# A hybrid decoder block: HGRN2's products inside blocks of 32 tokens in four partition ranges, and probabilities by values for two heads in turn

## The chip, the cores and the metric

The kernel runs on one core of a Trainium2 chip. The metric is the device time of one execution in microseconds (us), the median of three runs. All tensors are fp32; the large projections split each operand into a high and a low part and multiply those, so that each is several passes on TensorE. A matmul of fp32 operands shows as two MATMUL records and two LDWEIGHTS records in the trace (a product of 128x128 by 128x128 is one instruction in the code and two records).

## The reference, cut to what matters

One decoder layer on x (1024 tokens, 1024 wide): an RMSNorm, one combined projection, three groups of heads, an output projection, and a gated feed-forward part. The two groups that the change touches most:

```python
def hgrn2_mix(q, f_logit, i, g, lb, out_gain):      # 4 heads, keys and values 128 wide
    log_f = jnp.logaddexp(jnp.log(lb), jnp.log1p(-lb) + jax.nn.log_sigmoid(z))
    k = (1.0 - lb) * jax.nn.sigmoid(-z)
    ...
        b = jnp.cumsum(gc, axis=2)
        o_inter = jnp.einsum('bhck,bhkv->bhcv', qc * jnp.exp(b), S)
        decay = jnp.exp(jnp.where(causal[:, :, None], diff, -jnp.inf))
        A = jnp.einsum('bhtk,bhtsk,bhsk->bhts', qc, decay, kc)
        o = o_inter + jnp.einsum('bhts,bhsv->bhtv', A, vc)
        S = jnp.exp(b_last[:, :, 0, :])[..., None] * S + ...

def dsa_mix(...):                                    # 4 heads of 64, 256 keys kept per query
    logits = jnp.einsum('bqhd,bqkhd->bhqk', qb, kg) * (SA_DH ** -0.5)
    p = jax.nn.softmax(jnp.where(valid[:, None], logits, -jnp.inf), axis=-1)
    return jnp.einsum('bhqk,bqkhd->bqhd', p, vg)

x = x + (mixed @ w_out[layer]);  x = x + ((silu(a) * b) @ w_ffn_out[layer])
```

The third group, memory attention (`mem_mix`), is the same softmax attention over 256 memory tokens.

## The kernel before

Lines are those of the kernel before. A framework with a scheduler takes the program in the order of its code, simulates the engines, and sets from that the order in which each engine's queue holds its instructions; buffers come from pools by tag. PSUM has the tags `mm`, `lg`, `rc` and `sm`, two banks of 128x512 each; the large SBUF tiles are `x0` to `x17` and `m0` to `m7`, one buffer each.

The stages, by time in the trace: projections and the indexer's scores to 150 us; memory attention from there to about 280; the HGRN heads and, beside them, two bisections that find the 256th largest score of each query (blocks of queries 7 and 4 counted on VectorE, L635; blocks 6, 5, 3 and 2 on ScalarE, L632); sparse attention from about 553 to 703 with HGRN head 3 in front of it and among it; the output projection (`wo`) from 620 to 793; then the feed-forward part (`ff`, `fo`) to the end, which the change does not touch.

**HGRN levels.** A head is 1024 tokens in 8 chunks of 128. `hgrn_intra` (L504 to L554) builds A, the decayed products of keys and queries inside a chunk, by levels. Q (queries), K (keys) and F (decays) lie with the 128 key dimensions on the partitions and 1024 tokens along them. Level 0 is the diagonal; five more levels with w = 1, 2, 4, 8, 16 fill in the pairs that lie in opposite halves of a block of 2w tokens; w = 32 and 64 are done apart (L542). In each of the six products `level_products` (L511) multiplies all of a chunk's 128 keys by all of its 128 queries, 8 matmuls of 128x128 in two banks of `rc`, although a level uses only pairs at most 31 tokens apart. VectorE takes from it what belongs to the level: by a product with the identity (L528) for the diagonal and by `copy_predicated` under a mask (L535) for the others, each in two instructions of 128x512. Between the products `descend` scales Q on VectorE (L521), K on GpSimd (L522) and F on VectorE (L523), one half of the tokens at a time. So a level is a loop: matmuls read Q and K, then Q and K are overwritten, then the next level's matmuls read them.

Heads 0 to 2 run through `hgrn_intra` as the program order comes to them (279 to 330, 391 to 427, 459 to 513 us), among projections of other heads; head 3 is put among the sparse attention's steps by `fillers`, and its levels stand in front of nearly all of them (553 to 571 us).

**Sparse attention.** 32 items, one for each block b of 128 queries (7 down to 0) and head h. An item goes through logits (L819, L821), the exponential (L830), a scale by GpSimd (L836), transposes of the 128x128 blocks of probabilities on TensorE (L845) with copies to a tile `PT` (L848, L850), and `sa_out`: for each of the b+1 blocks of keys a matmul of 64 columns (L857) into partitions 0 to 63 (even head) or 64 to 127 (odd head) of a bank, and a copy of 64x128 by ScalarE (L859). The bank has the tag `mm` at first (tile names `sat_mm`) and `rc` later (`sat_rc`).

The memory attention's L711 does the same for its two blocks of memory tokens, head j outside and block kb inside.

Of the kernel before, what the change touches and what calls it, by code (L numbers as in the profile page):

```python
# [42 lines left out]
def hybrid_block(ctx, tc, xT, memT, wch, wikw, wv, wkm, wvm, woa, wob, wfi, wfo,  # L43
# [23 lines left out]
    def bank(tag):  # L67

        return pp.tile([128, 512], F32, tag=tag, name=nm(tag))
# [13 lines left out]
    def bs(b):  # L83
        return slice(b * 128, b * 128 + 128)
# [18 lines left out]
    lv = held(160).bitcast(U8).rearrange("p (a b) -> p a b", a=5)  # L103
# [196 lines left out]
    G.tensor_copy(lv, lvf)  # L300
# [203 lines left out]
    def hgrn_intra(h):  # L504
        s, Q, K, F, Gt, A = heads[h]
        idb = ident.unsqueeze(1).to_broadcast([128, 4, 128])

        def level_products(hf):
            rc = bank("rc")
            for c in range(4):  # L510
                T.matmul(rc[:, bs(c)], K[:, bs(4 * hf + c)], Q[:, bs(4 * hf + c)], start=True,  # L511
                         stop=True)
            return rc.rearrange("p (a b) -> p a b", a=4)
# [11 lines left out]
        lg = [level_products(hf) for hf in range(2)]  # L525
        for hf in range(2):
            V.tensor_mul(Q[:, hs(hf)], Q[:, hs(hf)], F[:, hs(hf)])
            V.tensor_mul(A[:, 4 * hf:4 * hf + 4], lg[hf], idb)  # L528
        yield
        for i in range(5):  # L530
            mask = lv[:, i, :].unsqueeze(1).to_broadcast([128, 4, 128])
            lg = [level_products(hf) for hf in range(2)]
            for hf in range(2):
                descend(1 << i, hf)
                V.copy_predicated(A[:, 4 * hf:4 * hf + 4], mask, lg[hf])  # L535
            yield
        for w in (32, 64):
# [139 lines left out]
    def memory_attention():  # L677
        ph[0] = "mat"
        Pm, PTm = mt(2, (128, 2, 2, 256)), mt(3, (128, 2, 2, 2, 128))
        for b in range(8):  # L680
            for m in range(2):
# [26 lines left out]
                for j in range(2):  # L708
                    h = 2 * m + j
                    for kb in range(2):  # L710
                        T.matmul(po[ROWS[j], 0:128], vm[:, kb, 64 * h:64 * h + 64], PT[:, j, kb, :],  # L711
                                 start=kb == 0, stop=kb == 1)
# [138 lines left out]

    def sa_out(t):
# [423 lines left out]
```

## Time and profile before

| | us |
|---|---|
| median of 3 runs | 1437.39 (1437.28 to 1437.59) |
| profiled execution, its own time | 1437.38 |
| span of that execution | 1435.6 |
| TensorE busy | 1331.7 (93%) |
| VectorE busy | 1062.5 (74%) |
| ScalarE busy | 685.2 (48%) |
| GpSimd busy | 462.4 (32%) |
| mean granted TensorE clock | 0.97 of full speed |

The profiled execution is 1.8 us longer than its span and agrees with the median to 0.01 us. In the rows below PE is TensorE, PEld its weight loads, DVE VectorE, ACT ScalarE, POOL GpSimd; Lnnn is a line of the kernel. "x16" in a row counts records; a busy TensorE includes the time that matmuls overlap one another, and a record's own duration says nothing of the rate, which is read from a burst's duration divided by its records. The share of 93% is a mean over stages with different limits: in one stage TensorE is busy without a gap, in the next it waits for VectorE.

### The profile page before, as it was taken

The page shows a single profiled execution, that of the slowest core. Times are in us where ns is not written, and L with a number is a line of the kernel's source. Part 1 is how long each engine was busy: PE and PEld are TensorE (multiplying, and loading weights), DVE is VectorE, ACT ScalarE, POOL GpSimd, SP SyncE. Part 2 cuts the span into 40 slices and gives each one's busy share as a digit, 9 for nine tenths or more (in the row PEclk, how much of TensorE's full clock was granted, in tenths as well). Part 3 has the DMA queues.
Part 4 walks back from the last instruction along what each step waited for, and adds up shares of the span by engine and source line. Part 5 has one row for each costly group of instructions (what it writes and reads, how often), then busy time and mean ns, then how long its engine had stood idle before and what let it go on. Part 6 is the DMA issues. An engine that isn't in the chain of part 4 may idle for free.

```text
span 1435.6 us, 19694 instructions
## 1 busy us (share of the span) xinstructions
PE 1331.7 (93%) x6920; PEld 1103.6 (77%) x6920; DVE 1062.5 (74%) x2119; ACT 685.2 (48%) x1350; POOL 462.4 (32%) x380
## 2 busy tenths in 40 slices
PE   7989999989999978999992999999999998899998
PEld 5767887779888867878771788888888886688887
DVE  8787998895496789654489578777777766666764
ACT  7565789857732252544543333333333333344442
POOL 1401034363365533211115133333332310903630
PEclk9999999999999997999995999999999999899999
DMA  6211011000101000011331232323333249543331
GB/s 229 74 30 30 16 45 31 30 22 27 56 17 45 19 18 32 31 34 48 103 118 58 74 109 97 103 102 103 103 110 110 97 138 352 197 165 101 103 110 59
DMA packets 50643, 120.08 MB, mean 84 GB/s; under 512 B 5744, under 2 KB 5872, under 8 KB 50544
## 3 DMA queue, kind: packets, MB, share of 16 engines
q1 hardware_dynamic: 50256, 118.61, 24.8%
q8 instruction: 54, 0.88, 0.3%
q14 instruction: 45, 0.37, 0.1%
q10 hardware_dynamic: 288, 0.22, 0.0%
HBM read 90.23 MB, written 28.57 MB: 83 GB/s over the span
## 4 chain that ended last, share of the span: by engine, by line
PE 64%; DVE 20%; ACT 9%; DMA 3%; issue 2%; POOL 0%; DVEq 0%; ACTq 0%; POOLq 0%; SPq 0%
PE ff_lg L1030 16%; PE ff_rc L1030 12%; PE wo_mm L184 4%; PE fo_mm L1172 4%; PE fo_sm L1172 4%; ACT idx_x L632 4%; PE fo_lg L1172 3%; PE fo_rc L1172 3%; DVE idx_x L635 3%; PE hg_mm L184 2%; PE sap_mm L184 2%; PE wo_mm L1006 2%; PE idx_mm L184 1%; PE mat_mm L184 1%; PE sat_rc L857 1%
## 5 line engine op out<-in xcount | busy, mean ns | idle before, releaser
L115 ACT ACTIVATE ff_whi<-ff_x 128x512 fp32r<-128x512 f32 x109 | 68.4, 630 | 125.7 <-PE ff_rc L1030 80.2
L1030 PE MATMUL ff_lg<-wo_h,ff_whi 128*128 128x512 f32 x440 | 127.0, 394 | 0.0
L632 ACT ACTIVATE idx_x<-idx_x,packs 128x896 int8<-128x896 f32 (+3 forms) x128 | 105.7, 826 | 44.1 <-DVE packs L627 39.4
L1030 PEld LDWEIGHTS ff_lg<-wo_h,ff_whi 128*128 128x128 f32 x440 | 82.5, 189 | 19.6 <-ACT ff_tmp L1036 2.9
L184 PE MATMUL hg_mm<-xn_h,hg_whi 128*128 128x512 f32 x384 | 96.7, 396 | 0.8 <-DVE hg_x L481 0.8
L1030 PE MATMUL ff_rc<-wo_x,ff_whi 128*128 128x512 f32 x264 | 80.9, 392 | 17.2 <-ACT wo_x L115 17.2
L116 DVE TENSOR_TENSOR ff_wlo<-ff_x,ff_whi 128x512 fp32r<-128x512 f32 x109 | 90.6, 832 | 6.4 <-PE ff_lg L1030 4.4
L1030 PE MATMUL ff_rc<-wo_h,ff_whi 128*128 128x512 f32 x264 | 83.4, 397 | 8.9 <-ACT ff_whi L115 6.6
L184 PEld LDWEIGHTS hg_mm<-xn_h,hg_whi 128*128 128x128 f32 x384 | 71.0, 189 | 15.4 <-DVE hg_x L481 1.0
L1030 PE MATMUL ff_lg<-wo_x,ff_whi 128*128 128x512 f32 x264 | 78.8, 391 | 0.0
L116 POOL TENSOR_TENSOR hg_wlo<-hg_wst,hg_whi 128x512 fp32r<-128x512 f32 x32 | 43.0, 1352 | 104.8 <-ACT hg_whi L115 79.1
L1030 PEld LDWEIGHTS ff_rc<-wo_x,ff_whi 128*128 128x128 f32 x264 | 49.8, 189 | 28.1 <-ACT wo_x L115 17.7
L635 DVE TENSOR_SCALAR_CACHE_REDUCE idx_x<-idx_x,packs 128x1024 int8<-128x1024 f32 x64 | 68.7, 1074 | 0.9
L1030 PE MATMUL ff_lg<-wo_h,ff_wlo 128*128 128x512 f32 x220 | 67.8, 389 | 0.0
L1030 PEld LDWEIGHTS ff_rc<-wo_h,ff_whi 128*128 128x128 f32 x264 | 50.2, 190 | 20.5 <-ACT ff_whi L115 7.0
L511 PE MATMUL hg_rc<-hg_x,hg_x 128*128 128x128 f32 x384 | 53.0, 289 | 11.2 <-POOL hg_x L522 5.7
L511 PEld LDWEIGHTS hg_rc<-hg_x,hg_x 128*128 128x128 f32 x384 | 49.4, 202 | 15.5 <-POOL hg_x L522 7.8
L522 POOL TENSOR_TENSOR hg_x<-hg_x,hg_x 128x256 f32<-128x256 f32 x56 | 45.4, 822 | 43.8 <-PE hg_rc L511 27.1
L1030 PEld LDWEIGHTS ff_lg<-wo_x,ff_whi 128*128 128x128 f32 x264 | 49.7, 188 | 10.7 <-ACT ff_whi L115 0.2
L836 POOL TENSOR_SCALAR sat_x<-sat_x,sat_mz 128x1024 f32<-128x1024 f32 (+7 forms) x32 | 24.1, 755 | 99.6 <-DVE sat_mz L835 80.1
L384 DVE SCALAR_TENSOR_TENSOR idx_x<-idx_tmp,packs,idx_x 128x512 f32<-128x512 f32 (+2 forms) x70 | 46.1, 711 | 12.3 <-ACT idx_tmp L379 11.9
L116 DVE TENSOR_TENSOR fo_wlo<-fo_tmp,fo_whi 128x512 fp32r<-128x512 f32 x33 | 33.5, 1017 | 26.4 <-ACT fo_whi L115 23.7
(445 smaller groups left out, 3722.6 us busy)
## 6 DMA issues: line engine op xcount, KB each, us to landing
gd<-ff_m SPq DMA_DIRECT2D x77, 256.0 KB, 2.0
fo_x<-gd SPq DMA_DIRECT2D x77, 256.0 KB, 3.0
ff_wst<-wfi SPq DMA_DIRECT2D x16, 512.0 KB, 3.6
ff_m<-wfi SPq DMA_DIRECT2D x14, 512.0 KB, 3.6
ff_x<-wfi SPq DMA_DIRECT2D x14, 512.0 KB, 3.7
hg_wst<-wch SPq DMA_DIRECT2D x12, 512.0 KB, 3.6
fo_x<-wfo SPq DMA_DIRECT2D x12, 512.0 KB, 6.4
fo_h<-wfo SPq DMA_DIRECT2D x20, 256.0 KB, 6.0
```

What stands on the lines that cost most here:

```text
L115: S.activation(hi, src, AF.Copy)
L116: (eng or V).tensor_sub(lo, src, hi.bitcast(F32))
L184: T.matmul(ps[:M, :], w(pw, k), h[p][k][hf], start=i == 0, stop=i == len(order) - 1)
L384: V.scalar_tensor_tensor(sc[b][:, c0:c1], rl[:, :c1 - c0], iww[:, b, h:h + 1], sc[b][:, c0:c1], op0=ALU.mult, op1=ALU.add)
L511: T.matmul(rc[:, bs(c)], K[:, bs(4 * hf + c)], Q[:, bs(4 * hf + c)], start=True, stop=True)
L522: G.tensor_mul(Kv[:, :, 0, :], Kv[:, :, 0, :], fr.to_broadcast([128, n, w]))
L632: S.activation(waste[S][:, :nk], sc[b], AF.Sign, bias=nf[:, j:j + 1], accum_out=ct[:, j:j + 1])
L635: eng.tensor_scalar(waste[eng][:, :nk], sc[b], fl[:, j:j + 1], None, op0=ALU.is_ge, op1=ALU.add, accum_out=ct[:, j:j + 1])
L836: G.tensor_scalar(P[:, :nk], P[:, :nk], mx[:, 2:3], 1.0, op0=ALU.mult, op1=ALU.mult)
L1006: T.matmul(ps, wb[k](pw, m), MX[p][KB[k]][hf], start=i == 0, stop=i == 8)
L1030: T.matmul(ps, w[pw][:, bs(k)], HB[u][k][p], start=first and i == 0, stop=i == 11, skip_group_check=True)
L1172: T.matmul(banks[m], w[i][pw][:, bs(m)], b[i][p], start=first and i == 0 and n == 0, stop=i == NP - 1 and n == 2, skip_group_check=True)
```

## The change

`level_products` keeps only what a level can use: for each chunk, four products of 32 keys by 32 queries, one for each block of 32 tokens. The four land in the four partition ranges 0-31, 32-63, 64-95, 96-127 of a PSUM bank, and one bank of 128 x (8x32) holds all eight chunks. There are 32 matmuls (64 records) a level where 8 (16 records) stood, and VectorE takes the level's part in one instruction of 128x256 instead of two of 128x512. After the last level three ScalarE copies a head move the blocks to their places in A and three GpSimd memsets clear what lies beside them. The masks shrink to 32 columns, and eight small copies on GpSimd set up masks and identity once.

In `sa_out` the even head of a pair only keeps its `PT`; the odd head then does both heads' products, alternating between them, and one copy of 128x128 instead of two of 64x128. `L711` alternates the two heads likewise.

```diff
-        idb = ident.unsqueeze(1).to_broadcast([128, 4, 128])
-        def level_products(hf):
+        Ad = A[:, :, 0:32]
+        def level_products():
             rc = bank("rc")
-            for c in range(4):
-                T.matmul(rc[:, bs(c)], K[:, bs(4 * hf + c)], Q[:, bs(4 * hf + c)], start=True,
-                         stop=True)
-            return rc.rearrange("p (a b) -> p a b", a=4)
+            for c in range(8):
+                for o in QUARTERS:
+                    sl = slice(128 * c + o.start, 128 * c + o.stop)
+                    T.matmul(rc[o, 32 * c:32 * c + 32], K[:, sl], Q[:, sl], start=True, stop=True)
+            return rc[:, :256].rearrange("p (c b) -> p c b", c=8)
...
-        lg = [level_products(hf) for hf in range(2)]
+        lg = level_products()
         for hf in range(2):
             V.tensor_mul(Q[:, hs(hf)], Q[:, hs(hf)], F[:, hs(hf)])
-            V.tensor_mul(A[:, 4 * hf:4 * hf + 4], lg[hf], idb)
+        V.tensor_mul(Ad, lg, wide(id32))
         yield
         for i in range(5):
-            mask = lv[:, i, :].unsqueeze(1).to_broadcast([128, 4, 128])
-            lg = [level_products(hf) for hf in range(2)]
+            lg = level_products()
             for hf in range(2):
                 descend(1 << i, hf)
-                V.copy_predicated(A[:, 4 * hf:4 * hf + 4], mask, lg[hf])
+            V.copy_predicated(Ad, wide(lv[:, i, :]), lg)
             yield
+        for o in QUARTERS[1:]:
+            S.activation(A[o, :, o], A[o, :, 0:32], AF.Copy)
+            G.memset(A[o, :, 0:o.start], 0.0)
...
-                for j in range(2):
-                    h = 2 * m + j
-                    for kb in range(2):
+                for kb in range(2):
+                    for j in range(2):
+                        h = 2 * m + j
                         T.matmul(po[ROWS[j], 0:128], vm[:, kb, 64 * h:64 * h + 64], PT[:, j, kb, :],
-                                 start=kb == 0, stop=kb == 1)
+                                 start=kb == 0, stop=kb == 1, skip_group_check=True)
...
     def sa_out(t):
-        b, h, PT, mx = t["b"], t["h"], t["PT"], t["mx"]
+        b, h = t["b"], t["h"]
         m, j = h // 2, h % 2
+        PTs[j] = t["PT"]
+        if j == 0:
+            return
         po = bank(po_tag[0])
         for kb in range(b + 1):
-            T.matmul(po[ROWS[j], 0:128], sv[kb // 4][:, kb % 4, 64 * h:64 * h + 64],
-                     PT[:, kb, :], start=kb == 0, stop=kb == b)
-        S.activation(M[4 + m][ROWS[j], bs(b)], po[ROWS[j], 0:128], AF.Copy)
+            for j in range(2):
+                T.matmul(po[ROWS[j], 0:128],
+                         sv[kb // 4][:, kb % 4, 128 * m + 64 * j:128 * m + 64 * j + 64],
+                         PTs[j][:, kb, :], start=kb == 0, stop=kb == b, skip_group_check=True)
+        S.activation(M[4 + m][:, bs(b)], po[:, 0:128], AF.Copy)
```

The scheduler places the new instructions. In the rows of order below, a row is the line, the operation, the tiles written and read and the shape; "x4" counts instructions of the same kind in a row. Lines of the changed kernel are some higher: L518 are the level products (L511 before), L527, L528 and L529 the descents (L521 to L523), L543 the `copy_predicated` (L535), L546 and L547 the new copies and memsets, L553 the products of w = 32 and 64 (L542), L678 to L686 the steps after the bisections (L667 to L675), L856 the transposes (L845), L875 the products of probabilities and values (L857).

TensorE before, at the end of head 3's levels and the start of sparse attention's output; the rows are of the kernel before.

```order
L511 MATMUL hg_rc_5492<-hg_x_659_4037,hg_x_660_4038 128x128 x4
L511 MATMUL hg_rc_5497<-hg_x_659_4037,hg_x_660_4038 128x128 x4
L845 MATMUL sat_sm_5312<-packs,sat_x_777_5237 128x128 x4
L845 MATMUL sat_sm_5318<-packs,sat_x_777_5237 128x128 x4
L542 MATMUL hg_rc_5583<-hg_x_659_4037,hg_x_660_4038 32x32 x16
L857 MATMUL sat_mm_5370<-sat_x_793_5311,sap_x_557_3000 64x128 x4
L857 MATMUL sat_mm_5370<-sat_x_793_5311,sap_x_558_3001 64x128 x4
```

TensorE at the same place in the changed kernel.

```order
L518 MATMUL hg_rc_6011<-hg_x_641_4458,hg_x_642_4459 32x32 x32
L553 MATMUL hg_rc_6129<-hg_x_641_4458,hg_x_642_4459 32x32 x8
L856 MATMUL sat_sm_5777<-packs,sat_x_759_5658 128x128 x4
L856 MATMUL sat_sm_5783<-packs,sat_x_759_5658 128x128 x4
L553 MATMUL hg_rc_6129<-hg_x_641_4458,hg_x_642_4459 32x32 x8
L553 MATMUL hg_rc_6197<-hg_x_641_4458,hg_x_642_4459 64x64 x4
L856 MATMUL sat_sm_5845<-packs,sat_x_764_5706 128x128 x4
L875 MATMUL sat_mm_5925<-sat_x_773_5776,sap_x_551_3145 64x128
L856 MATMUL sat_sm_5851<-packs,sat_x_764_5706 128x128 x4
```

A level is one burst of 32 small matmuls into one bank, where two times four large ones into two banks stood. The first product of a pair stands by itself among the transposes, before the second head's `PT` is there; a few rows on the rest follow, alternating between the two heads' tiles:

```order
L856 MATMUL sat_sm_5913<-packs,sat_x_769_5761 128x128 x4
L875 MATMUL sat_mm_5925<-sat_x_781_5844,sap_x_551_3145 64x128
L875 MATMUL sat_mm_5925<-sat_x_773_5776,sap_x_551_3145 64x128
L875 MATMUL sat_mm_5925<-sat_x_781_5844,sap_x_551_3145 64x128
L875 MATMUL sat_mm_5925<-sat_x_773_5776,sap_x_551_3145 64x128
```

Every matmul of the pair but the first is next to one of the other head, where a head's whole run stood alone before.

VectorE before, at the end of head 1's levels, where the bisection's last scores are scanned (L672, 896 columns).

```order
L521 TENSOR_TENSOR hg_x_505_2630<-hg_x_505_2630,hg_x_507_2632 128x32x8
L535 COPY_PREDICATED hg_x_530_2820<-packs,hg_rc_3489 128x512
L670 TENSOR_SCALAR packs<-packs 128x1
L523 TENSOR_TENSOR hg_x_507_2632<-hg_x_507_2632 128x32
L521 TENSOR_TENSOR hg_x_505_2630<-hg_x_505_2630,hg_x_507_2632 128x16x16
L535 COPY_PREDICATED hg_x_530_2820<-packs,hg_rc_3502 128x512
L523 TENSOR_TENSOR hg_x_507_2632<-hg_x_507_2632 128x16
L672 SCALAR_TENSOR_TENSOR idx_x_155_801<-idx_x_158_804 128x896
L673 SCALAR_TENSOR_TENSOR idx_x_155_801<-idx_x_155_801,packs,idx_x_158_804 128x896
L674 SCALAR_TENSOR_TENSOR idx_x_155_801<-idx_x_156_802,idx_x_155_801 128x896
L521 TENSOR_TENSOR hg_x_505_2630<-hg_x_505_2630,hg_x_507_2632 128x16x16
L535 COPY_PREDICATED hg_x_530_2820<-packs,hg_rc_3507 128x512
```

VectorE there in the changed kernel (L683 to L685 are the scan and what follows it).

```order
L678 TENSOR_SCALAR idx_x_156_809,packs<-idx_x_155_808,packs 128x896
L527 TENSOR_TENSOR hg_x_499_2775<-hg_x_499_2775,hg_x_501_2777 128x16x16 x2
L543 COPY_PREDICATED hg_x_524_2965<-packs,hg_rc_3757 128x8x32
L681 TENSOR_SCALAR packs<-packs 128x1
L529 TENSOR_TENSOR hg_x_501_2777<-hg_x_501_2777 128x16 x2
L683 SCALAR_TENSOR_TENSOR idx_x_155_808<-idx_x_158_811 128x896
L684 SCALAR_TENSOR_TENSOR idx_x_155_808<-idx_x_155_808,packs,idx_x_158_811 128x896
L685 SCALAR_TENSOR_TENSOR idx_x_155_808<-idx_x_156_809,idx_x_155_808 128x896
L527 TENSOR_TENSOR hg_x_499_2775<-hg_x_499_2775,hg_x_501_2777 128x8x32 x2
```

The last level (w = 16) stands whole in front of the scan, where its second half stood behind the scan and its two followers.

GpSimd before at the same place.

```order
L669 TENSOR_SCALAR idx_x_158_804<-idx_x_155_801,packs 128x896
L522 TENSOR_TENSOR hg_x_506_2631<-hg_x_506_2631,hg_x_507_2632 128x32x8
L522 TENSOR_TENSOR hg_x_506_2631<-hg_x_506_2631,hg_x_507_2632 128x16x16
L669 TENSOR_SCALAR idx_x_158_804<-idx_x_156_802,packs 128x768
L522 TENSOR_TENSOR hg_x_506_2631<-hg_x_506_2631,hg_x_507_2632 128x16x16
L522 TENSOR_TENSOR hg_x_506_2631<-hg_x_506_2631,hg_x_507_2632 128x8x32
```

GpSimd there in the changed kernel.

```order
L680 TENSOR_SCALAR idx_x_158_811<-idx_x_155_808,packs 128x896
L528 TENSOR_TENSOR hg_x_500_2776<-hg_x_500_2776,hg_x_501_2777 128x16x16 x2
L547 MEMSET hg_x_524_2965 32x8x32
L547 MEMSET hg_x_524_2965 32x8x64
L547 MEMSET hg_x_524_2965 32x8x96
L680 TENSOR_SCALAR idx_x_158_811<-idx_x_156_809,packs 128x768
L528 TENSOR_TENSOR hg_x_500_2776<-hg_x_500_2776,hg_x_501_2777 128x8x32 x2
```

The three memsets stand behind the last level's descent and in front of the second L680 and of the descent of w = 32.

## Rows read from the trace of the kernel before

**Rows 1.** The page's first part: busy us, share of span, instructions.
```profile
PE 1331.7 (93%) x6920; PEld 1103.6 (77%) x6920; DVE 1062.5 (74%) x2119; ACT 685.2 (48%) x1350; POOL 462.4 (32%) x380
```

**Rows 2.** Windows by stage: busy us of each engine, granted clock, DMA.
```profile
core 0: us, PE busy (x) PEld busy (x) DVE busy (x) ACT busy (x) POOL busy (x), PEclk, DMA share, GB/s
280.00:330.00 50.00, 42.60 (x263) 38.02 (x261) 49.58 (x111) 26.90 (x59) 28.83 (x23) 0.97 0.11 32
...
391.00:427.00 36.00, 31.48 (x286) 30.28 (x284) 32.25 (x72) 13.12 (x31) 21.31 (x18) 0.99 0.10 30
427.00:517.00 90.00, 89.22 (x545) 77.05 (x544) 65.36 (x164) 24.09 (x43) 41.45 (x39) 0.99 0.10 29
...
553.00:571.00 18.00, 14.66 (x99) 12.97 (x98) 16.62 (x51) 3.79 (x6) 7.72 (x10) 0.92 0.00 0
571.00:607.00 36.00, 36.00 (x305) 31.11 (x306) 26.62 (x86) 19.69 (x39) 12.45 (x14) 1.00 0.08 23
...
625.00:703.00 78.00, 77.57 (x413) 61.19 (x411) 33.35 (x107) 37.15 (x95) 10.51 (x19) 1.00 0.19 58
```

**Rows 3.** Chain of waits, head 0: start, us, engine, tile, line.
```profile
287.11 0.60 DVE hg_x L528
...
293.61 0.67 DVE hg_x L535
```

**Rows 4.** Chain of waits, end of head 1.
```profile
416.45 2.41 DVE idx_x L672
...
420.29 3.16 issue
423.46 0.65 POOL hg_x L522
```

**Rows 5.** Chain of waits, head 2.
```profile
492.01 1.78 PE hg_rc L511 x16
...
498.34 0.63 PE hg_rc L542 x32
...
502.35 1.07 PE hg_rc L542 x16
```

**Rows 6.** Chain of waits, head 3.
```profile
553.60 1.72 PE hg_rc L511 x8
...
558.50 0.34 DVE hg_x L521
558.84 0.67 DVE hg_x L535
...
569.56 1.32 POOL sat_x L836
```

**Rows 7.** Windows, TensorE alone at the start of head 3.
```profile
553.00:556.00 3.00, 3.00 (x15) 0.51 0.00 0
```

**Rows 8.** Groups of GpSimd by shape: count, busy us, mean ns, idle.
```profile
L522 POOL TENSOR_TENSOR hg_x<-hg_x,hg_x 128x256 f32<-128x256 f32 x56 | 45.4, 822 | 43.8 <-PE hg_rc L511 27.1 <-PE hg_rc L542 12.6 <-DVE hg_x L521 2.4
...
L836 POOL TENSOR_SCALAR sat_x<-sat_x,sat_mz 128x768 f32<-128x768 f32 x4 | 3.6, 909 | 13.9 <-DVE sat_mz L835 11.6 <-DVE sat_mz L825 1.7 <-DVE hg_abx L148 0.7
```

**Rows 9.** Windows, line 857 alone (probabilities by values).
```profile
571.00:607.00 36.00, 14.80 (x114) 12.15 (x114) 1.00 0.08 23
607.00:625.00 18.00, 6.80 (x54) 5.35 (x54) 1.00 0.14 47
625.00:703.00 78.00, 17.27 (x120) 12.32 (x120) 1.00 0.19 58
```

**Rows 10.** Chain of waits, one such burst.
```profile
572.84 1.89 PE sat_mm L857 x16
```

**Rows 11.** Timeline of TensorE, memory attention: start, us, line, tiles, records.
```profile
204.13 0.66 PE L711 MATMUL mat_sm<-mat_m,mkv_x 128*64 128x128 f32 x8
204.72 1.21 PE L184 MATMUL hg_mm<-xn_h,hg_whi 128*128 128x512 f32 x4
```

**Rows 12.** Lines, ScalarE's copies of wider ranges: min/median/max ns.
```profile
L547 ACT ACTIVATE hg_x<-hg_rc x12: 356/374/591, 333.7 to 577.7; 32x256 f32<-32x256 f32 x8, 64x512 f32<-64x512 f32 x4
```

More of the change, by code (lines that the diff above doesn't have):

```diff
@@ L102, in hybrid_block @@
     vs, cs = held(V_END), held(C_END)
-    lv = held(160).bitcast(U8).rearrange("p (a b) -> p a b", a=5)
+    lv = held(40).bitcast(U8).rearrange("p (a b) -> p a b", a=5)
+    id32 = held(32)
+    QUARTERS = [slice(o, o + 32) for o in range(0, 128, 32)]
     S.dma_start(vs, vec)
@@ L299, in hybrid_block @@
     nc.sync.dma_start(lvf, lvl)
-    G.tensor_copy(lv, lvf)
+    for o in QUARTERS:
+        G.tensor_copy(lv[o], lvf[o, :, o])
+        G.tensor_copy(id32[o], ident[o, o])
     mT = [xt(6 + i, [128, 4, 256]) for i in range(2)]
@@ L505, in hgrn_intra @@
         s, Q, K, F, Gt, A = heads[h]
-        idb = ident.unsqueeze(1).to_broadcast([128, 4, 128])
-        def level_products(hf):
+        Ad = A[:, :, 0:32]
+        def level_products():
             rc = bank("rc")
-            for c in range(4):
-                T.matmul(rc[:, bs(c)], K[:, bs(4 * hf + c)], Q[:, bs(4 * hf + c)], start=True,
-                         stop=True)
-            return rc.rearrange("p (a b) -> p a b", a=4)
+            for c in range(8):
+                for o in QUARTERS:
+                    sl = slice(128 * c + o.start, 128 * c + o.stop)
+                    T.matmul(rc[o, 32 * c:32 * c + 32], K[:, sl], Q[:, sl], start=True, stop=True)
+            return rc[:, :256].rearrange("p (c b) -> p c b", c=8)
         def descend(w, hf):
@@ L523, in descend, with wide @@
             V.tensor_mul(fl, fl, fr)
-        lg = [level_products(hf) for hf in range(2)]
+        def wide(t):
+            return t.unsqueeze(1).to_broadcast([128, 8, 32])
+        lg = level_products()
         for hf in range(2):
             V.tensor_mul(Q[:, hs(hf)], Q[:, hs(hf)], F[:, hs(hf)])
-            V.tensor_mul(A[:, 4 * hf:4 * hf + 4], lg[hf], idb)
+        V.tensor_mul(Ad, lg, wide(id32))
         yield
         for i in range(5):
-            mask = lv[:, i, :].unsqueeze(1).to_broadcast([128, 4, 128])
-            lg = [level_products(hf) for hf in range(2)]
+            lg = level_products()
             for hf in range(2):
                 descend(1 << i, hf)
-                V.copy_predicated(A[:, 4 * hf:4 * hf + 4], mask, lg[hf])
+            V.copy_predicated(Ad, wide(lv[:, i, :]), lg)
             yield
+        for o in QUARTERS[1:]:
+            S.activation(A[o, :, o], A[o, :, 0:32], AF.Copy)
+            G.memset(A[o, :, 0:o.start], 0.0)
         for w in (32, 64):
@@ L850, in sa_turn @@
                 V.tensor_copy(PT[:, g0:g1, :], tv)
+    PTs = {}
     def sa_out(t):
-        b, h, PT, mx = t["b"], t["h"], t["PT"], t["mx"]
+        b, h = t["b"], t["h"]
         m, j = h // 2, h % 2
+        PTs[j] = t["PT"]
+        if j == 0:
+            return
         po = bank(po_tag[0])
         for kb in range(b + 1):
-            T.matmul(po[ROWS[j], 0:128], sv[kb // 4][:, kb % 4, 64 * h:64 * h + 64],
-                     PT[:, kb, :], start=kb == 0, stop=kb == b)
-        S.activation(M[4 + m][ROWS[j], bs(b)], po[ROWS[j], 0:128], AF.Copy)
+            for j in range(2):
[3 more added lines that the diff above has]
+        S.activation(M[4 + m][:, bs(b)], po[:, 0:128], AF.Copy)
     def pipeline(items, stages):
```

## The prediction, made before the changed kernel had run

> **What bounds the kernel now.** The page first: TensorE is busy 93% of the span [rows 1]. That is a mean, so the windows by stage come next, to see in which of the changed stages TensorE is full and in which it waits [rows 2]. Head 0 (280 to 330): VectorE is busy 49.58 of 50 us, TensorE 42.60. Head 1 (391 to 427): neither is full, 32.25 and 31.48 of 36. Head 2 (427 to 517): TensorE 89.22 of 90, since projections fill its waits. Head 3 (553 to 571): VectorE 16.62 of 18. Sparse attention: TensorE full, 36.00 of 36 from 571 and 77.57 of 78 from 625. The chain of waits, read third, says the same by instruction: in heads 0 and 3 it runs through VectorE's pieces (L528, L535 and the descents) [rows 3, 6], in head 2 through L511 itself [rows 5]. So one edit has several prices: where VectorE bounds, what it no longer reads counts; where TensorE is full, the matmuls count.
>
> **The change, part by part.** The sum is made against the profiled execution, 1437.38 us (span 1435.6 and 1.8 around it), which is 0.01 us under the median of the runs.
>
> *VectorE's share of a level.* A piece of 128x512 costs 0.60 us (L528) or 0.67 us (L535) on the chain [rows 3]; a piece of 128x256 costs 0.34 us (L521) [rows 6]. A head had two L528 and ten L535, and now has one and five at half the width: 2 x 0.60 + 10 x 0.67 = 7.9 us becomes 6 x 0.36 = 2.2 us (0.36 as the row's 0.34 and a little, since L535 is longer than L528 too), so 5.7 us a head are gone. In head 0 VectorE is the bound and TensorE has 7 us of slack, which the shorter bursts widen. What comes next there is GpSimd, 28.83 of 50 [rows 2], so I take 5 of the 5.7; at the worst 2, if the bisection's other half (ScalarE's counts, whose small steps stand in VectorE's queue) sets the pace.
>
> *Head 1.* Its first part waits for the bisection on ScalarE, which the change does not touch; from 404 on VectorE leads. Of the pieces behind that only some five L535 remain, 5 x 0.67 against 3 x 0.36 us. VectorE's order puts all of the last level in front of the scan of 2.41 us (L672), where before its second half came behind the scan, L673 and L674; the chain shows 3.16 us of issue and then the GpSimd descent that waited for it [rows 4]. Against that, three memsets now stand in GpSimd's queue in front of the second L680. I take 2.5 us gained, between 0 and 5.
>
> *Head 2.* TensorE is full, so a burst of L511 costs what it lasts: 1.78 us, six times [rows 5]. The trace has no burst into four ranges. The nearest row is L542 for w = 32, the same tiles into two ranges: 32 records in 0.63 us, 20 ns each, the switches to and from narrow tiles included. Sixty-four records cost 0.63 us if four ranges run beside one another as two do, and 1.26 if they gain nothing over two. I take the middle, 0.95: 6 x 0.83 = 5.0 us, between 3.1 and 6.9.
>
> The Trainium skill says something against this in "TensorE: Matmul & The Clock Gate" (Wait — 56ns, not 53.3ns?): start-to-start never drops below about 25 ns, however small the product is. By that 64 records take an estimated 1.6 us, head 2 gains 1.1 instead of 5.0, and the sum would be 4 us smaller. The row of 20 ns a record stands below that floor, so I go by the row.
>
> *Head 3.* Here VectorE's pieces follow one another from 555 to 570; it loses 5.7 of its 16.62 us. Then GpSimd's descents come near: ten at 0.82 us [rows 8], 8.2 us in sequence, and each level's burst has to wait for them. The first burst runs at half clock and takes 1.72 us for 8 records [rows 6, 7]; the new one is shorter there too, if not in proportion. I take 4.5 us, between 0 (the loop TensorE to GpSimd to TensorE sets the pace) and 6.
>
> *Probabilities by values.* L857 is busy 14.80, 6.80 and 17.27 us in three stretches [rows 9], and a burst of one head alone goes at 1.89 us for 16 records, 118 ns each [rows 10]. For two heads' halves beside one another the nearest row is the memory attention's L711, whose halves follow one another closely in the same way: the next matmul starts 0.59 us after the first of 8 records, 74 ns each [rows 11]. If alternating does no better than that, a record saves 37%; at full overlap (59 ns) 50%. I use 45%: 6.7, 3.1 and 7.8 us of TensorE. From 571 to 607 TensorE falls to some 29 us against VectorE's 26.62 and the order puts the first product of a pair alone in front of the transposes, so 5 of 6.7; from 607 to 625 VectorE and ScalarE share the stretch with it, 1; from 625 the products stand between long runs of `wo_mm` that keep TensorE full, but the short items at the end go from engine to engine, so 4. Together 10 us, between 3 (VectorE takes over) and 17 (all of it).
>
> *Where I cost nothing.* The L711 edit: the trace already has 74 ns there, and that stage hangs on the bisection; at 59 ns its 128 records would give TensorE 1.9 us in a place where it is not waited for. The eight small set-up copies: GpSimd idles in that stage; without that cover they cost about a microsecond. Sixteen ScalarE copies fewer in sparse attention: ScalarE is at 37.15 of 78 there.
>
> *What is added.* Three ScalarE copies a head at 0.37 us [rows 12], which only the products of A by values much later wait for. Three memsets of 256, 512 and 768 elements a head; the trace has no such memset, and the nearest row, a scale of 768 elements, takes 0.91 us [rows 8], so at most some 2 us a head in GpSimd's queue, and near nothing if a memset is cheap. Behind them wait the descent of w = 32 and, in head 3, a scale of the probabilities (L836) and through it TensorE's transposes. For block 7 only two `PT` tiles exist, so the transposes of the next item wait until a pair is out. Together I put 1 us against the gain, between 0 and 4.
>
> The sum: -5 - 2.5 - 5 - 4.5 - 10 + 1 = -26 us; 1437.4 - 26 = 1411.4. **Forecast: 1411 us.**
>
> **The rivals.**
>
> *A. Half is lost to the next bound.* GpSimd's descents in heads 0 and 3 and VectorE in sparse attention take over: -2 in head 0, 0 in head 1, -4 in head 2, -1.5 in head 3, -4.5 in sparse attention, +2 for what is added: -10, so 1427. For it: VectorE at 26.62 of 36 and GpSimd's 0.82 us. Against it: in heads 0 and 3 GpSimd idles 43.8 us in front of its descents, most of it waiting for L511 [rows 8], which gets shorter.
>
> *B. All of it lands*: -5.7 - 5 - 6.9 - 6 - 14 = -37.6, 1400. For it: 625 to 703 really is full of TensorE work. Against it: head 1 hangs on ScalarE until 404.
>
> *C. TensorE's clock.* In front of head 3 the granted clock is 0.51, the 1.2 GHz level, after a stretch in which TensorE mostly waited [rows 7]; in head 3 as a whole it is 0.92 [rows 2]. If smaller bursts with more waiting leave TensorE at the lower level through head 3 and into the sparse attention, head 3's gain goes and the first ten microseconds of sparse attention cost some 3 us more: -26 + 4.5 + 3 = -18, 1419. Against it: 0.97 and 0.99 in heads 0 and 1, where TensorE also waits.
>
> *D. Slower: ranges do not run beside one another.* One range alone costs 67 ns a record in the w = 64 burst, 16 in 1.07 us [rows 5]; the w = 32 row allows up to 40 if its two ranges fully share. Then a level takes 2.6 to 4.3 us instead of 1.78, in 24 bursts, and head 2 loses from 28 ns a record on. At 67 ns the bursts add 15 us to each head, and with the slack of rows 2: +8 in head 0, +10 in head 1, +15 in head 2, +10 in head 3, nothing for sparse attention: 1480. At 40 ns it is -2, -1, +5, 0 and 0: 1439. The middle is 1460. The change as a whole turns slower at about 40 ns. Against it: 20 ns in the w = 32 row, twice what one range's pace would allow if nothing overlapped.
>
> **How the numbers follow.** The forecast's own case 0.62, A 0.20, B 0.08, C 0.05, D 0.04; the last 0.01 is for no change. What a measurement of this kernel can tell from no change is about 0.2%, 2.9 us, so faster means under 1434.5. That holds for the first four cases but for a little of A: faster 0.92, same 0.03 (the edges of A and D), slower 0.05. The range of 8 in 10 runs from B's edge, 1398, to just past A, 1429.
>
> **What would show it.** In the profile after: bursts of L518 (64 records) between 0.6 and 1.3 us and about 0.95 in head 2; L543 at 0.36 to 0.38 us, five a head; heads 0 and 3 about 5 us shorter each; pairs of L875 at 59 to 74 ns a record instead of 118; everything behind 793 us unchanged in length. The prediction is wrong if L518's record costs over 28 ns, if GpSimd's descents (L528) lead the chain in heads 0 and 3, or if the pairs of L875 take as long as the two heads did apart.

## The result and the profile after

The changed kernel takes 1418.7 us (median of 4 runs, 1417.05 to 1418.80) against 1437.49 us for the kernel before on the same chip: a ratio of 0.9864, 95% interval 0.9852 to 0.9876, 18.8 us less. The forecast was 1411, its range 1398 to 1429. The direction and the range held; 7 us of the 26 did not come.

The profiled execution took 1418.78 us (span 1417.0). Its windows, cut where the heads' bursts begin and end in this trace (columns as in [rows 2]: busy time and count of TensorE, its weight loads, VectorE, ScalarE and GpSimd, then TensorE's granted clock, DMA share, GB/s):

```profile
280.80:331.50 50.70, 42.13 (x593) 35.73 (x592) 47.69 (x108) 28.40 (x62) 30.62 (x24) 0.87 0.10 32
...
457.80:488.00 30.20, 30.20 (x498) 24.24 (x498) 23.31 (x37) 7.75 (x13) 20.58 (x21) 1.00 0.11 31
...
546.20:562.00 15.80, 7.69 (x401) 6.30 (x400) 14.96 (x46) 2.69 (x5) 8.28 (x10) 0.61 0.01 2
562.00:598.00 36.00, 35.49 (x309) 29.57 (x309) 26.47 (x92) 22.07 (x44) 14.49 (x18) 0.91 0.06 19
```

Head 0 still fills VectorE (47.69 of 50.70 us), though by the forecast's sum 5.7 us of work were taken from it. Head 3 is shorter than its 18 us in [rows 2], but TensorE's clock in it has fallen from 0.92 to 0.61. Read between the same events in both traces (first and last record of the level bursts, the end of the last count of ScalarE's bisection, the last product of probabilities and values; the bursts and products by their starts), the 18.6 us between the two spans are made so. The 2.9 us from VectorE's last instruction to the end of the span are the same in both:

| stretch | before, us | after, us | change | forecast |
|---|---|---|---|---|
| start to the end of ScalarE's bisection (head 0 in it) | 404.1 | 407.2 | +3.1 | -5 |
| from there to head 2's first burst (head 1 in it) | 55.5 | 50.6 | -4.9 | -2.5 |
| head 2, first to last burst | 33.9 | 28.3 | -5.6 | -5 |
| head 2's last to head 3's first burst | 59.9 | 60.2 | +0.3 | 0 |
| head 3, first to last burst | 16.4 | 14.0 | -2.4 | -4.5 |
| head 3's last burst to the last product of sparse attention | 133.1 | 124.3 | -8.8 | -10 |
| from there to the end of VectorE's last instruction | 729.8 | 729.4 | -0.4 | 0 |

The first two rows belong together: head 2 begins 1.8 us earlier, where the forecast had 7.5, and that is most of what did not come.

The new bursts, TensorE's records of the level products alone (L518, columns: busy time of TensorE and of its weight loads, clock, DMA), and the pairs in the chain of waits (start, duration, records), to be read beside [rows 5, 10]:

```profile
457.00:487.00 30.00, 4.58 (x384) 3.91 (x384) 1.00 0.10 31
...
546.20:562.00 15.80, 6.95 (x384) 5.76 (x384) 0.61 0.01 2
```

```profile
570.00 1.02 PE sat_mm L875 x16
...
608.23 1.46 PE sat_rc L875 x24
```

Six bursts of 64 records keep TensorE busy for 4.58 us in head 2, 0.76 us each, the last record's own 0.2 us included; from the first record's start to the last one's it is 0.57 us, 9 ns a record. In head 3 the same records take 6.95 us. A pair's product costs 64 or 61 ns a record where it was 118.

VectorE and the new work (columns of the first: minimum, median, maximum ns; of the memsets: busy us, mean ns):

```profile
L543 DVE COPY_PREDICATED hg_x<-packs,hg_rc x20: 425/434/451, 293.8 to 561.4; 128x256 f32<-128x256 uint8 x20
```

```profile
L546 ACT ACTIVATE hg_x<-hg_x x12: 412/414/417, 331.7 to 564.0; 32x256 f32<-32x256 f32 x12
```

```profile
L547 POOL MEMSET hg_x<- 32x768 f32 x4 | 2.9, 733 | 0.2
L547 POOL MEMSET hg_x<- 32x512 f32 x4 | 2.1, 519 | 0.2
L547 POOL MEMSET hg_x<- 32x256 f32 x4 | 1.3, 325 | 6.8 <-ACT hg_x L546 6.6
```

The narrow `copy_predicated` is as cheap as forecast (0.43 us in itself; the next instruction starts 0.33 us after it in most places). What lies around it is not. This is head 3, level w = 1, VectorE and GpSimd in order of time (start, duration, line, operation; the waits for another engine in brackets):

```profile
548.52 1.64 POOL L528 TENSOR_TENSOR hg_x<-hg_x,hg_x 128x256 f32<-128x256 f32 x2 [11.65 <-PE hg_rc L518]
548.66 0.75 DVE L149 SCALAR_TENSOR_TENSOR sap_abx<-sap_abx 128x32 f32<-128x32 f32 x1
549.33 1.10 DVE L527 TENSOR_TENSOR hg_x<-hg_x,hg_x 128x256 f32<-128x256 f32 x1
550.36 0.18 DVE L150 TENSOR_TENSOR sap_abx<-sap_abx 128x32 f32<-128x32 f32 x1
550.46 0.42 DVE L527 TENSOR_TENSOR hg_x<-hg_x,hg_x 128x256 f32<-128x256 f32 x1
...
551.38 0.83 POOL L528 TENSOR_TENSOR hg_x<-hg_x,hg_x 128x256 f32<-128x256 f32 x1 [1.22 <-DVE hg_x L529]
551.46 0.80 DVE L151 SCALAR_TENSOR_TENSOR sap_abx<-sap_abx 128x32 f32<-128x32 f32 x1
552.18 0.41 DVE L529 TENSOR_TENSOR hg_x<-hg_x 128x256 f32<-128x256 f32 x1
```

An instruction of 128x32 takes 0.18 us where GpSimd is idle and 0.75 or 0.80 us beside a descent of GpSimd; a descent of VectorE takes 0.42 and 1.10. Each of the long ones begins while a descent of GpSimd runs, and ends as that one ends or up to 0.3 us after it. No row shows a wait, for it lies inside the instruction's own time and counts as busy. The `copy_predicated`, which reads PSUM, does not do this: its longest of 20 is 0.451 us, its shortest 0.425. Seven of the 20 lie wholly inside a GpSimd instruction (0.429 to 0.441 us), eight beside none (0.430 to 0.440). Of the 56 descents of Q on VectorE (L527, 0.41 us at the least) the 14 that began while GpSimd was idle took 0.41 to 0.43 us; the 14 that took over 0.43 all began inside a GpSimd instruction. The other 28 began inside one as well and took no longer: 13 in its last 0.06 us, eight beside the comparisons of L680, six beside memsets and one beside a descent. The kernel before, at the same place:

```profile
558.63 0.91 POOL L522 TENSOR_TENSOR hg_x<-hg_x,hg_x 128x256 f32<-128x256 f32 x1 [0.17 <-PE hg_rc L511]
558.76 0.74 DVE L535 COPY_PREDICATED hg_x<-packs,hg_rc 128x512 f32<-128x512 uint8 x1
...
559.39 0.19 DVE L148 TENSOR_TENSOR sap_abx<-sap_abx 128x32 f32<-128x32 f32 x1
559.51 0.41 DVE L523 TENSOR_TENSOR hg_x<-hg_x 128x256 f32<-128x256 f32 x1
```

There the wide copy filled the 0.9 us of GpSimd's descent, and the instructions behind it ran at their short times. The sum over head 3 can be read at the ten small instructions that VectorE has between the levels there (tile sap_abx): from the head's first burst to its last they take 2.63 us before and 5.07 after, and 2.39 us for 13 of them in E3 below, where GpSimd does no descent (window, its length, busy time and count on VectorE, TensorE's clock, DMA, GB/s; before, after, E3):

```profile
553.39:569.75 16.36, 2.63 (x10) 0.92 0.00 1
546.29:560.31 14.02, 5.07 (x10) 0.62 0.01 2
532.25:544.76 12.51, 2.39 (x13) 0.77 0.02 4
```

So the theory for the experiments: what the copies gave up in head 0 and 3, VectorE's other instructions spent again waiting out GpSimd.

### The profile page after: what moved, and what is told of

It is laid out like the page before. It is cut to its first block, busy times and chain, and to the rows that moved or that the text cites. A ratio compares the mean times of both kernels' runs of the same rounds, so it can differ in the third digit from the quotient of the medians.

```text
span 1417.0 us, 21980 instructions
## 1 busy us (share of the span) xinstructions
PE 1303.6 (92%) x8072; PEld 1069.1 (75%) x8072; DVE 1052.7 (74%) x2095; ACT 685.7 (48%) x1346; POOL 474.1 (33%) x399
## 4 chain that ended last, share of the span: by engine, by line
PE 58%; DVE 7%; DMA 2%; POOL 2%; issue 1%; ACT 1%; SPq 0%; DVEq 0%; POOLq 0%; ACTq 0%
PE ff_lg L1049 17%; PE ff_rc L1049 12%; PE wo_mm L186 4%; PE fo_mm L1191 4%; PE fo_sm L1191 4%; PE fo_lg L1191 3%; PE fo_rc L1191 3%; PE sap_mm L186 2%; PE wo_mm L1025 2%; PE hg_mm L186 2%; PE sat_sm L856 1%; PE sat_lg L830 1%; DMA fo_x<-wfo 1%; DMA fo_h<-wfo 1%; DVE wo_h L118 1%
## 5 line engine op out<-in xcount | busy, mean ns | idle before, releaser
L528 POOL TENSOR_TENSOR hg_x<-hg_x,hg_x 128x256 f32<-128x256 f32 x56 | 48.4, 879 | 30.5 <-PE hg_rc L518 15.1
L186 PE MATMUL hg_mm<-xn_h,hg_wlo 128*128 128x512 f32 x192 | 50.9, 397 | 0.0
L1144 POOL TENSOR_TENSOR fo_tmp<-fo_x,fo_h 128x512 f32<-128x512 f32 x20 | 30.8, 1559 | 52.5 <-DVE fo_wlo L118 52.5
```

Source lines behind the costliest of these rows:

```text
L186: T.matmul(ps[:M, :], w(pw, k), h[p][k][hf], start=i == 0, stop=i == len(order) - 1)
L528: G.tensor_mul(Kv[:, :, 0, :], Kv[:, :, 0, :], fr.to_broadcast([128, n, w]))
L1144: G.tensor_add(t, a21, a22)
```

## The experiments

All are compared with the kernel before on the same chip. "The changed kernel" is the 1418.7 us one.

**The two edits apart.** E1 takes the level products alone, E2 the pairs alone.

```diff
 E1: the changed kernel with sa_out and the memory attention's loop as before
 E2: the kernel before with
-        for kb in range(b + 1):
-            T.matmul(po[ROWS[j], 0:128], ... 64 * h:64 * h + 64], PT[:, kb, :], ...)
+        PTs[j] = t["PT"]
+        if j == 0:
+            return
...
+        for kb in range(b + 1):
+            for j in range(2):
+                T.matmul(po[ROWS[j], 0:128], ... PTs[j][:, kb, :], ...)
```

Expected of E1: 

> The changed kernel with the level products alone: probabilities by values and the memory attention's loop are those of before. By the milestones of the two traces the levels gave about 9.5 us and the pairs about 9.5. Theory (the two edits add up): 1428, and the stretch from the first logits product after head 3 to the output projection as long as before. Rival (the level edit takes TensorE's clock from the sparse attention, and the pairs hide that): sparse attention is longer than before by 3 us or more, 1431.

Expected of E2: 

> The kernel before with the pairs alone (sa_out and the memory attention's loop). Theory (the two edits add up): 1428, all of it gained between 571 and 703 us, a burst of a pair at 60 to 75 ns a record. Rival (the clock that the level edit lowers costs the sparse attention 3 us): the pairs alone gain 12 or more, 1425. Second rival: the memory attention's loop gives something too, and the stretch before 280 us is a microsecond shorter.

E1: 1433.5 us, ratio 0.9963 (0.9948 to 0.9978), 4 us gained. E2: 1424.9 us (1421.21 to 1427.64), ratio 0.9913 (0.9897 to 0.9930), 13 us gained (10 to 15 by its interval). The pairs are worth at least the 10 forecast by themselves, the levels far less than 17. In E1 head 3's last burst is 9.6 us earlier than before (560.1 against 569.7), but the last product of sparse attention only 3.7 us (699.1 against 702.8). Behind head 3, E1's windows and E2's:

```profile
546.20:562.00 15.80, 7.57 (x401) 6.22 (x400) 14.72 (x47) 2.90 (x5) 9.65 (x10) 0.61 0.01 2
562.00:567.00 5.00, 4.91 (x38) 4.07 (x39) 3.93 (x15) 3.60 (x9) 4.83 (x8) 0.50 0.02 3
```

```profile
550.00:566.00 16.00, 13.03 (x97) 11.42 (x96) 15.68 (x47) 2.67 (x5) 6.31 (x9) 1.00 0.00 1
566.00:569.00 3.00, 2.10 (x44) 1.63 (x42) 3.00 (x9) 1.71 (x3) 3.00 (x4) 1.00 0.00 0
```

With the narrow bursts TensorE is busy 7.57 of 15.80 us in head 3 with a granted clock of 0.61, and the first 5 us of sparse attention run at 0.50, the 1.2 GHz level; with the wide ones it is busy 13.03 of 16 and stays at 1.00. The rival of both runs has the better of it: the levels take something from the sparse attention. From head 3's last burst to the last product it is 139.0 us in E1 against 133.1 before, and 121.5 in E2. That the clock is the reason is not shown by these two runs. In E2 the stretch before 280 us is 0.8 us shorter in the profiled execution, too little to credit to the memory attention's loop.

**Is it GpSimd?** E3 puts the keys' descent on VectorE, in all heads; E8 in head 0 alone.

```diff
-            G.tensor_mul(Kv[:, :, 0, :], Kv[:, :, 0, :], fr.to_broadcast([128, n, w]))
+            V.tensor_mul(Kv[:, :, 0, :], Kv[:, :, 0, :], fr.to_broadcast([128, n, w]))
 E8: (V if h == 0 else G).tensor_mul(...)
```

Expected of E3: 

> The changed kernel with the keys' descent on VectorE instead of GpSimd, 14 instructions of 128x256 more on VectorE a head, at 0.34 us 4.8 us. Theory (VectorE's instructions on SBUF operands wait out GpSimd's descent inside their own time, so what VectorE saved by the narrower copies went into that): head 3's levels do not get longer than the 14.0 us of the changed kernel, the small instructions of 128x32 in it go back to 0.2 us, head 0 within 2 us of the 44.2 it takes from its first to its last burst; 1417 to 1421. Rival (VectorE simply has too much work): head 0 and head 3 each 4 us longer, 1427.

Expected of E8: 

> The changed kernel with the keys' descent on VectorE in head 0 alone. With it in all heads the time was 1405, head 0 took 37.0 us from first to last burst instead of 45.1, the bisection on ScalarE ended at 402 instead of 407, and head 2 began at 445 instead of 458. Theory (head 0 lost its gain to instructions that wait out GpSimd, and it is there that the bisection's steps are held up): the bisection ends at 402 to 404, the whole 1413 to 1415. Rival (the gain is made in head 1 and behind it, where GpSimd's queue holds the descents and the low parts of the weights): head 0 shorter and the bisection's end where it was, 1418.

E3: 1405.1 us, ratio 0.9769 (0.9755 to 0.9784): more work for the fuller engine, and 13.5 us less than the changed kernel. Head 0 takes 37.0 us from first to last burst instead of 45.1, head 3 12.5 instead of 14.0. VectorE in E3's head 3, with GpSimd idle:

```profile
535.08 0.18 DVE L151 SCALAR_TENSOR_TENSOR sap_abx<-sap_abx 128x32 f32<-128x32 f32 x1
535.18 0.42 DVE L527 TENSOR_TENSOR hg_x<-hg_x,hg_x 128x256 f32<-128x256 f32 x1
535.52 0.42 DVE L528 TENSOR_TENSOR hg_x<-hg_x,hg_x 128x256 f32<-128x256 f32 x1
535.85 0.18 DVE L149 SCALAR_TENSOR_TENSOR sap_abx<-sap_abx 128x32 f32<-128x32 f32 x1
```

Every instruction is back at its short time. The time went below the theory's own 1417 to 1421 (which counted head 0 at 44.2 us; by the records it is 45.1), and E8 says where the rest is: 1412.1 us, ratio 0.9827 (0.9813 to 0.9840), 6.6 us from head 0 alone and 1 us below its own theory's range, with the bisection's end at 401.9 instead of 407.2, as that theory had it.

Head 0's 8 us, however, are for the most part not the wait. In the changed kernel the selection of block 4 (L678 to L685, 6.1 us of VectorE, 317 to 326 us) stands between head 0's bursts; in E3, in E8 and in E4 below the scheduler has put it behind them. And by ScalarE's count that begins at 327.9 us in the changed kernel, E3 (327.9) and E8 (327.2) have gained next to nothing. The gain is made in the two counts behind the next one: 14.5 us in the changed kernel (333.0 to 347.5), 10.4 in E3 and E8, 12.1 in the kernel before. What stands there in the changed kernel:

```profile
338.04 2.79 POOL L118 TENSOR_TENSOR hg_wlo<-hg_wst,hg_whi 128x512 fp32r<-128x512 f32 x2 [1.34 <-ACT hg_whi L117]
338.09 1.26 DVE L655 SCALAR_TENSOR_TENSOR packs<-packs 128x4 int32<-128x4 int32 x1
...
341.03 1.04 ACT L643 ACTIVATE idx_x<-idx_x,packs 128x896 int8<-128x896 f32 x1 [1.93 <-DVE hg_x L529]
```

A step of the bisection on four numbers takes 1.26 us beside GpSimd's low part of the weights, and ScalarE sits idle for 1.93 us in front of its next count. In the kernel before the same steps took 0.17 us each and were through 0.4 us before the low part began; in E3 and E8 it lies between such steps. So it is the same wait, but beside another instruction than the descent, and how much of E8's gain is the descent's own and how much the new order's is not told apart.

The other 7 us lie around head 1: from the bisection's end to head 2's first burst E8 takes 51.1 us, E3 42.6. The chain of the changed kernel there goes through GpSimd's queue:

```profile
410.70 2.77 POOL hg_wlo L118 x2
413.47 1.92 issue
415.45 2.54 POOL idx_x L680
418.01 2.47 DVE idx_x L683
420.50 1.36 DVE idx_x L684
421.91 0.73 POOL hg_x L547
422.73 2.58 POOL idx_x L680
425.31 2.63 POOL hg_x L528 x2
```

In front of the descent of w = 32 (L528) stand the two L680 and the memsets, the order that the prediction priced with the memsets. Here the descent itself is what E3 takes out of the queue; that this makes the whole difference was argued from the chain and not tested by itself.

**Was it there before?** E9 makes E3's edit on the kernel before, with no part of the change.

```diff
-            G.tensor_mul(Kv[:, :, 0, :], Kv[:, :, 0, :], fr.to_broadcast([128, n, w]))
+            V.tensor_mul(Kv[:, :, 0, :], Kv[:, :, 0, :], fr.to_broadcast([128, n, w]))
```

> The kernel before (no part of the change), with the keys' descent on VectorE instead of GpSimd. On the changed kernel the same edit gave 13.5 us. Theory (in the kernel before, the wide copies read PSUM and ran beside GpSimd's descents, so that little was waited for; the descent on GpSimd became dear only with the narrow copies): little or nothing gained, since VectorE now pays 4.8 us a head in heads 0 and 3 where it bounds; 1433 to 1442. Rival (GpSimd is the wrong engine for it in either kernel): 13 us gained here too, 1424.

1447.4 us, ratio 1.0061 (1.0048 to 1.0073): 9 us slower, a little beyond the theory's range and on the other side from its rival. The same edit costs 9 us with the wide copies and gives 13.5 with the change. That the descent was well placed on GpSimd in every head does not follow. Heads 0 and 1 get shorter in E9 as well (44.2 and 27.6 us from first to last burst, 47.7 and 30.8 before). Head 2 takes 2.0 us more, and head 3, which begins 7.4 us earlier, 24.9 instead of 16.4: twelve records of the sparse attention's L821 stand on VectorE among its levels, where the kernel before has none. The scheduler's order changed with the edit, and the two are not told apart.

**Do the copies hide the wait?** E4 does each narrow copy twice.

```diff
             for hf in range(2):
                 descend(1 << i, hf)
-            V.copy_predicated(Ad, wide(lv[:, i, :]), lg)
+                V.copy_predicated(Ad, wide(lv[:, i, :]), lg)
```

> The changed kernel with each level's copy_predicated done twice, once behind each half's descent (the same values again): five more instructions of 128x256 a head, 1.8 us of VectorE. Theory (these copies run beside GpSimd's descent while the other instructions wait for it, so that they cost little): heads 0 and 3 within 0.7 us of the changed kernel's, 1418 to 1420. Rival (the copies are paid in full where VectorE bounds): 1.8 us more in heads 0 and 3 each and some in head 1, 1423.

1423.5 us, ratio 0.9893 (0.9878 to 0.9908), 5 us slower than the changed kernel: the rival's number. Head 3 pays 1.6 of its 1.8 us (15.6 against 14.0), so there the copies hid next to none of it. The bisection's end stays where it was (406.8 against 407.2), but the order changed in front of it: head 0's bursts take 38.9 us with five copies more, since the selection of block 4 has moved behind them. Another 3.7 us go between the bisection's end and head 2 (54.3 against 50.6), where the order of head 1 changed too. So the theory is not borne out: only in head 2, where TensorE is full, did the copies cost nothing (28.3 us both times).

**Four ranges at once.** E6 sends neighbours in the queue to the same range.

```diff
-            for c in range(8):
-                for o in QUARTERS:
+            for o in QUARTERS:
+                for c in range(8):
```

> The changed kernel with the level products in another order: all eight chunks of one partition range, then the next range, so that neighbours in TensorE's queue write the same range. A burst of 64 records takes 0.57 us in head 2 of the changed kernel, 9 ns a record. Theory (four ranges work beside one another, and one range alone is about four times as slow): 25 to 40 ns a record, 1.6 to 2.6 us a burst, head 2 6 to 12 us longer; 1428 to 1440 with the heads that wait for more than TensorE. Rival (a record of 32 columns simply is that short, whatever range it goes to): 0.57 us again, 1419.

1433.7 us, ratio 0.9978 (0.9969 to 0.9987): 15 us lost. A burst in head 2's chain:

```profile
468.86 1.84 PE hg_rc L518 x64
```

The burst is longer than the 1.78 us of the old one [rows 5]. From the first record's start to the last one's, as above, it is 1.72 us instead of 0.57 in each of head 2's six bursts: 27 ns a record instead of 9. The count of the records and their width are the same; what makes them short is that neighbours go to different ranges. Head 3 takes 27.6 us instead of 14.0; there halves of a level can no longer follow one another either, since every range's pass reads all eight chunks, and twelve records of the sparse attention's L832 stand on VectorE among its levels, none in the changed kernel. These are not told apart.

**The clock in head 3.** E5 puts extra matmuls, whose result nothing reads, in front of head 3's bursts; E7 does so on E3.

```diff
             rc = bank("rc")
+            if h == 3:
+                for _ in range(6):
+                    T.matmul(rc[:, 256:512], qst[0][0][:, 0:128], kst[0][0][0][:, 0:256],
+                             start=True, stop=True)
```

Expected of E5: 

> The changed kernel, with six extra matmuls of 128x256 in front of each of head 3's six level bursts, into the unused half of the burst's bank, so that TensorE works while it waits for the descent. In the changed kernel the granted clock is 0.61 in head 3 and 0.50 in the 5 us behind it, where the kernel before had 0.92 and 1.00. Theory (the level edit lets TensorE fall to 1.2 GHz, and that costs the head's bursts and the first sparse items): the clock in and behind head 3 is over 0.9, a burst of 64 falls from 1.2 to 0.6 us, the stretch from the last burst to the first product of probabilities falls from 6.8 us to about 4; 1414 to 1416. Rival (the clock does not matter, since VectorE and GpSimd set the pace there): no gain, 1419, or the extra matmuls stand in the way, 1421.

Expected of E7: 

> The keys' descent on VectorE (1405 us by itself) and the extra matmuls in head 3 together. Theory (two separate costs of the changed kernel): both gains add, 1401 to 1403. Rival (with VectorE in front of every burst TensorE's clock is not waited for): 1405.

E5: 1419.5 us (1415.41 to 1421.05), ratio 0.9875 (0.9859 to 0.9890); E7: 1404.0 us, ratio 0.9771 (0.9758 to 0.9784). Neither differs from the kernel it was made from. E5's windows of TensorE (last three: clock, DMA share, GB/s):

```profile
548.00:551.00 3.00, 2.71 (x107) 2.20 (x106) 3.00 (x8) 0.00 (x0) 1.83 (x2) 1.00 0.00 0
551.00:554.00 3.00, 1.67 (x61) 1.49 (x65) 3.00 (x9) 0.00 (x0) 1.59 (x2) 0.95 0.02 5
554.00:557.00 3.00, 2.57 (x69) 2.17 (x62) 3.00 (x10) 0.00 (x0) 1.80 (x3) 0.50 0.00 0
...
563.00:568.00 5.00, 5.00 (x66) 3.68 (x65) 4.74 (x18) 2.84 (x8) 4.75 (x8) 0.91 0.02 3
```

The extra work raised the clock in the head's first part and behind it, but not from 554 to 563, so the clock that the theory asked for was not reached. The first product of sparse attention came 3.1 us earlier (564.0 against 567.1), the last 0.8 us (683.8 against 684.6). In E7 it is 4.6 and 1.2 us. Most of an earlier start is given back inside the sparse attention; what then holds it was not tested.

**One more move.** E10, on E3, places the diagonal blocks by GpSimd instead of ScalarE.

```diff
-            S.activation(A[o, :, o], A[o, :, 0:32], AF.Copy)
+            G.tensor_copy(A[o, :, o], A[o, :, 0:32])
```

> The changed kernel with the keys' descent on VectorE, and the three copies a head that place the diagonal blocks on GpSimd instead of ScalarE. Theory (ScalarE's bisection sets the pace until 402 us, and three copies of 0.41 us stand in its queue): 1.2 us less until the bisection's end, 1403 to 1404. Rival (GpSimd's copies make VectorE's instructions wait, as the descents did): 1405 to 1408.

1406.0 us (1403.87 to 1409.86), ratio 0.9779 (0.9765 to 0.9794), no different from E3. The bisection ended at 401.9 us, 0.6 earlier than in E3, but head 0 had begun 1.7 us earlier there.

The best version is the change with the keys' descent on VectorE (E3): 0.9769, 33 us under the kernel before.

## Why the prediction was right, and where it was not

*Head 2*: right. The burst was priced at 0.95 us between 0.63 and 1.26 and takes 0.57 to 0.76; 5.6 us gained for 5.0.

The floor of about 25 ns a record that "TensorE: Matmul & The Clock Gate" of the Trainium skill states (Wait — 56ns, not 53.3ns?) would have made it an estimated 1.6 us. The trace's 9 ns disagrees where neighbours write different ranges; E6's 27 ns, with neighbours in one range, does not contradict it.

*Sparse attention*: right in kind, and the term too small by itself: 61 to 64 ns a record, inside the forecast's 59 to 74 [rows 10, 11], and E2 gained 13 us for 10. In the whole change it shows 8.8, since the levels take something from it (E1). Head 3's clock is the likely reason but not a shown one: E5 raised it only in part, and that stretch went from 124.3 to 122.8 us.

*Head 0*: the step that failed. "I take 5 of the 5.7; at the worst 2": the bisection ended 3.1 us later. Of these, 1.2 us lie in front of head 0's first burst. From there to ScalarE's count at 327.9 us the change gained 0.9 us, and 2.8 us were lost behind it, 2.0 of them at the step shown above. The copies became cheaper as computed, but the sum treated VectorE's other instructions as fixed lengths, and beside GpSimd they stretch. VectorE from head 0's first burst to that count (window, its length, busy time and count, clock, DMA, GB/s): the copies before and after, then the descent of F (L523, L529) before and after:

```profile
279.57:327.58 48.01, 5.84 (x8) 0.96 0.11 33
280.79:327.89 47.10, 1.74 (x4) 0.87 0.11 35
279.57:327.58 48.01, 3.06 (x8) 0.96 0.11 33
280.79:327.89 47.10, 5.95 (x8) 0.87 0.11 35
```

Eight instructions of the same shapes take 2.9 us more, over half of what the copies gave up. The copies from PSUM were among those that do not stretch: 23 of the 40 wide ones lay wholly inside a GpSimd instruction, at 0.72 to 0.75 us like the others. That they covered the wait fits the two traces; E4, which puts copies back, does not bear it out. The prediction's own worst case, ScalarE's counts setting the pace, is what held behind head 0's bursts.

Rival A named GpSimd as the next bound at the right place, but by its own 0.82 us in sequence. The price was paid inside VectorE's busy time, where neither the windows nor the waits show it; so GpSimd's descents hardly lead the chain in head 3, though they set its pace. The 43.8 us of idle time that A was answered with [rows 8] are all four heads'; in heads 0 and 3 they are 4.6 and 19.2. The stretching could have been seen in the trace before, where one form of a VectorE descent ranged from 0.40 to 1.51 us (columns: minimum, median, maximum ns, first and last start):

```profile
L521 DVE TENSOR_TENSOR hg_x<-hg_x,hg_x x56: 399/420/1510, 293.1 to 578.8; 128x256 f32<-128x256 f32 x56
```

The Trainium skill has the mechanism in "SBUF — State Buffer" (SBUF: two separate sides): VectorE, when it reads two operands in SBUF or runs in one of its two-port modes, and GpSimd take one pair of ports in turn, whoever starts first for its whole instruction. The traces agree, the 0.75 to 1.10 us in head 3 above all, but not everywhere: beside L680, which reads SBUF too, eight of nine descents of VectorE were not held (0.41 to 0.42 us). The prediction did not weigh that rule.

*Head 1*: 4.9 us gained for 2.5, inside its range. Part of it may be luck: the bisection ended late, and what did not wait for it went on meanwhile.

*Head 3*: 2.4 for 4.5. The ten small instructions alone take 2.4 us more, and E3 gives it back (12.5 us). Rival C's clock came too, 0.61 in the head, where C had expected it. C's 4.5 + 3 us were too dear; E5 and E7 recovered 3 to 5 us of start and next to nothing of the total. That C's sum, 1419, is the measured time is chance: it leaves head 0 its 5 us.

*Rival D* was wrong for this kernel and right as a mechanism: E6 is that case, at 27 ns a record. It is 15 us slower than the changed kernel and still 4 us under the kernel before; the prediction put the break-even at 40 ns, which no run tried.

*Additions*: 0.41 us a copy and 1.58 us of memsets a head, as bounded. What they delay is small: in head 0 ScalarE's next count begins 0.4 us late behind the three copies, and in head 1 a memset of 0.73 us stands in the chain shown above. E10 took the copies off ScalarE and won nothing.

## What to carry to other kernels

Small products into different partition ranges of one bank, issued in turn, cost a third of the large ones here (0.57 us a level against 1.67 to 1.90, from first to last start); issued range by range (1.72 us) they cost as much. An engine's busy time can hold waits for another engine: before counting what a cheaper instruction saves, compare the shortest and longest time of its neighbours, and ask which instruction was covering for which. When an edit shortens one of two engines that work on the same memory, try the other engine's share on it again: here the same move cost 9 us before the change and gave 13 after it. Where a scheduler sets the order, compare the order too before a difference is put down to the edit: it moved the selection in E3, E4 and E8 and the sparse attention's steps in E6 and E9.

## What the runs showed of the hardware

- Products of 32 columns: 9 ns a record over four ranges in turn, 27 ns in one range after another (start to start, in the changed kernel and in E6).
- A VectorE instruction on two SBUF operands of 128x32 lasts 0.18 us alone and up to 0.82 us beside a GpSimd descent, one of 128x4 up to 1.26 us beside a longer one; one that reads PSUM (`copy_predicated`, 128x256) stayed within 0.425 to 0.451 us in all 20 places.
- Two heads' halves in turn: 61 to 64 ns a record against 118 apart.
